# Seven own-buffer column pieces and seeded dot products at the end of a streaming matrix-vector kernel with a running record count

## Chip, cores, metric

One core of one Trainium2 chip. The metric is the device time of one execution in microseconds. PE is TensorE, PEld its weight load, DVE is VectorE, ACT is ScalarE, POOL is GpSimd, SP issues the input loads.

## The reference

```python
B, S, D = 8, 2048, 4096
x: (B, S, D) float32, w: (D, 1) float32

proj = (x @ w).squeeze(-1)                 # (8, 2048)
cm = np.maximum.accumulate(proj, axis=1)   # running maximum
is_record = (proj >= cm)
return np.cumsum(is_record, axis=1)        # how many records so far
```

The input is 268.4 MB and each element is used once. Whatever else the kernel does, it has to pull that much through the DMA engines.

## The kernel before

Positions lie on partitions. Seven groups of 256 positions are loaded as tiles of 128 partitions by 2 positions (32 KB per partition, 4 MB per load), the last 256 positions as two groups of 128 (2 MB per load), each group for all eight batches. DVE makes a dot product per position with one instruction that multiplies and sums. A transpose on PE then brings the sums of a group to a row per batch, and three short DVE instructions do the scan.

```python
const_pool = ctx.enter_context(tc.tile_pool(name="const", bufs=1))
xpool = ctx.enter_context(tc.tile_pool(name="xpool", bufs=4))     # [P, 2*D] each, 32 KB per partition
...
LAST = {                                  # how the last two tiles are cut into column pieces
    1: [(1024, D), (0, 1024)],
    0: [(2048, D), (768, 2048), (0, 768)],
}
...
parts = const_pool.tile([P, 32], FP32)    # the last small tile allocated before the x buffers
...
        if not split:                     # all groups but the last
            for j in range(r):
                xs = x_sb[:, j * D : (j + 1) * D]
                nc.vector.scalar_tensor_tensor(
                    out=xs, in0=xs, scalar=1.0, in1=w_sb, op0=ALU.mult, op1=ALU.mult,
                    accum_out=sum_v[:, j * B + b : j * B + b + 1])
        else:                             # last group: DVE takes columns below 3072 ...
            ...
            if c1 > CV:                   # ... Pool and ACT the 1024 above
                xp = x_sb[:, CV - c0 : c1 - c0]
                nc.gpsimd.tensor_mul(out=xp, in0=xp, in1=w_sb[:, CV:c1])
                nc.scalar.activation(out=xp, in_=xp, func=ACTF.Copy, accum_out=sum_p[:, b : b + 1])
            if b and c1 < D:
                nc.gpsimd.tensor_add(out=sum_v[:, b : b + 1], in0=sum_v[:, b : b + 1], in1=acc_v)
...
                for k, (m, lhs) in enumerate(mms):     # transposes; the piece sums of batch 0 are added here
                    nc.tensor.matmul(out=ps[:m, j : r * P : r], lhsT=lhs, rhs=identity, ...)
```

Every piece of the last two tiles goes into one of the same four 32 KB buffers, so a piece cannot be loaded before an older tile has been worked off.

Of the kernel before, what the change touches and what calls it, by code (L numbers as in the profile page):

```python
# [12 lines left out]
FP32 = mybir.dt.float32  # L13
ALU = mybir.AluOpType
ACTF = mybir.ActivationFunctionType
# [3 lines left out]
@with_exitstack  # L19
def kernel(  # L20
    ctx: ExitStack,
    tc: tile.TileContext,
    x: bass.AP,
    w: bass.AP,
    out: bass.AP,
):






    nc = tc.nc
    P = 128
    B, S, D = x.shape
    CV = 3072
    NW = 8
    WC = D // NW

    const_pool = ctx.enter_context(tc.tile_pool(name="const", bufs=1))  # L40
    xpool = ctx.enter_context(tc.tile_pool(name="xpool", bufs=4))
    gpool = ctx.enter_context(tc.tile_pool(name="gpool", bufs=2))
    wpsum = ctx.enter_context(
        tc.tile_pool(name="wpsum", bufs=1, space=bass.MemoryType.PSUM)
    )
    psum_pool = ctx.enter_context(
        tc.tile_pool(name="psum", bufs=2, space=bass.MemoryType.PSUM)
    )

    LAST = {  # L50
        1: [(1024, D), (0, 1024)],
        0: [(2048, D), (768, 2048), (0, 768)],
    }
    groups = []
    s = 0
    while s < S:
        r = 2 if s + 4 * P <= S else 1
        groups.append((s, r))
        s += r * P
    NG = len(groups)  # L60
    loads = []
    for g in range(NG):
        for b in reversed(range(B)):
            cuts = LAST.get(b) if g == NG - 1 else None
            for c0, c1 in cuts or [(0, D)]:
                loads.append((g, b, c0, c1))

    def start_load(i):
        g, b, c0, c1 = loads[i]
        s, r = groups[g]  # L70
        x_sb = xpool.tile([P, 2 * D], FP32, name="x_sb")
        if r == 2:
            nc.sync.dma_start(
                out=x_sb,
                in_=x[b, s : s + 2 * P, :].rearrange("(p r) d -> p (r d)", r=2),
            )
        else:
            nc.sync.dma_start(out=x_sb[:, : c1 - c0], in_=x[b, s : s + P, c0:c1])
        return x_sb

    AHEAD = 2
    first = [start_load(i) for i in range(AHEAD)]

    w_row = const_pool.tile([NW, WC], FP32)
    nc.scalar.dma_start(out=w_row, in_=w.rearrange("(k c) one -> k (c one)", k=NW))
    identity = const_pool.tile([P, P], FP32)
    make_identity(nc, identity)
    w_v = wpsum.tile([P, CV], FP32)
    w_sb = const_pool.tile([P, D], FP32)
    for k in range(NW):  # L90
        c = k * WC
        if c < CV:
            dst = w_v[:, c : c + WC]
        else:
            dst = psum_pool.tile([P, WC], FP32, name="ps")
        nc.tensor.matmul(  # L96
            out=dst, lhsT=identity[:NW, k : k + 1].to_broadcast([NW, P]),
            rhs=w_row, start=True, stop=True,
        )
        nc.scalar.copy(out=w_sb[:, c : c + WC], in_=dst)  # L100

    neg = const_pool.tile([B, 2 * P], FP32)
    zero = const_pool.tile([B, 2 * P], FP32)
    nc.gpsimd.memset(neg, NEG)
    nc.gpsimd.memset(zero, 0.0)
    parts = const_pool.tile([P, 32], FP32)

    state = {"cm": NEG, "cnt": 0.0}

    def scan_group(g, ps):  # L110
        s, r = groups[g]
        n = r * P
        cm = gpool.tile([B, n], FP32, name="cm")
        rec = gpool.tile([B, n], FP32, name="rec")
        cnt = gpool.tile([B, n], FP32, name="cnt")
        nc.vector.tensor_tensor_scan(  # L116
            out=cm, data0=ps[:B, :n], data1=neg[:, :n], initial=state["cm"],
            op0=ALU.max, op1=ALU.max,
        )
        nc.vector.tensor_tensor(out=rec, in0=ps[:B, :n], in1=cm, op=ALU.is_ge)  # L120
        nc.vector.tensor_tensor_scan(  # L121
            out=cnt, data0=rec, data1=zero[:, :n], initial=state["cnt"],
            op0=ALU.add, op1=ALU.add,
        )
        state["cm"] = cm[:, n - 1 : n]
        state["cnt"] = cnt[:, n - 1 : n]
        eng = nc.sync if g == NG - 1 else nc.scalar
        eng.dma_start(out=out[:, s : s + n], in_=cnt)

    pending = None  # L130
    npart = 0
    late = []
    for i, (g, b, c0, c1) in enumerate(loads):
        s, r = groups[g]
        x_sb = first[i] if i < AHEAD else start_load(i)
        split = g == NG - 1
        if b == B - 1:
            sum_v = gpool.tile([P, 2 * B], FP32, name="sum_v")
            sum_p = gpool.tile([P, B], FP32, name="sum_p")
        if not split:  # L140
            for j in range(r):
                xs = x_sb[:, j * D : (j + 1) * D]
                nc.vector.scalar_tensor_tensor(  # L143
                    out=xs, in0=xs, scalar=1.0, in1=w_sb,
                    op0=ALU.mult, op1=ALU.mult,
                    accum_out=sum_v[:, j * B + b : j * B + b + 1],
                )
        else:
            acc_v = sum_v[:, b : b + 1]
            if c1 < D:  # L150
                acc_v = parts[:, npart : npart + 1]
                late.append((b, acc_v))
                npart += 1
            v1 = min(c1, CV)
            if v1 > c0:
                xs = x_sb[:, : v1 - c0]
                nc.vector.scalar_tensor_tensor(  # L157
                    out=xs, in0=xs, scalar=1.0, in1=w_v[:, c0:v1],
                    op0=ALU.mult, op1=ALU.mult, accum_out=acc_v,
                )  # L160
            if c1 > CV:
                xp = x_sb[:, CV - c0 : c1 - c0]
                nc.gpsimd.tensor_mul(out=xp, in0=xp, in1=w_sb[:, CV:c1])  # L163
                nc.scalar.activation(  # L164
                    out=xp, in_=xp, func=ACTF.Copy, accum_out=sum_p[:, b : b + 1]
                )
            if b and c1 < D:
                nc.gpsimd.tensor_add(
                    out=sum_v[:, b : b + 1], in0=sum_v[:, b : b + 1], in1=acc_v
                )  # L170
        if pending is not None and b == B - 3:
            scan_group(*pending)
            pending = None
        if b == 0 and c0 == 0:
            ps = psum_pool.tile([P, WC], FP32, name="ps")
            for j in range(r):
                mms = [(B, sum_v[:, j * B : (j + 1) * B])]
                if split:
                    mms.append((B, sum_p))
                    mms.extend((1, col) for lb, col in late if lb == 0)  # L180
                for k, (m, lhs) in enumerate(mms):
                    nc.tensor.matmul(  # L182
                        out=ps[:m, j : r * P : r], lhsT=lhs, rhs=identity,
                        start=k == 0, stop=k == len(mms) - 1,
                    )
            pending = (g, ps)
    scan_group(*pending)
# [30 lines left out]
```

## Time and profile before

| what | before | read from |
|---|---|---|
| time | 634.01 us median of 4 (633.93 to 634.09) | runs |
| span of the profiled execution | 632.0 us | page |
| input | 268.4 MB at about 432 GB/s | slice table |
| one 128x4096 dot product | 4417 ns, 120 of them | groups |
| step from one 4 MB load to the next | 9.67 us (median) | completions in the trace |
| time of one 32 KB packet | 1213 ns (7139 of 7168 packets) | packets in the trace |
| last whole 2 MB load landed | 615.30 us | completions |
| last piece landed | 626.13 us | completions |
| last matmul ends | 628.38 us | timeline |

The page of the kernel before: the 40 equal slices of the span (the DMA row is the mean busy share of the 16 DMA engines in tenths) and the group of the full-width dot products (busy us, mean ns | idle before).

```profile
DVE  0699999989899889999899898998989989999976
DMA  9999999999999999999999999999999999999994
GB/s 370 438 438 436 438 436 432 431 432 431 431 432 431 431 431 432 431 431 436 433 436 438 438 436 430 432 436 431 431 431 432 431 433 433 427 431 431 431 429 178
...
L143 DVE SCALAR_TENSOR_TENSOR x_sb<-x_sb,w_sb 128x4096 f32<-128x4096 f32 x120 | 524.6, 4417 | 50.4 <-DMA x_sb<-in_x_dram 29.1
```

The DMA engines are full from start to end. DVE is busy 90% of the time but is not the limit: two dot products take 8.7 us (they start 4.35 us apart where DVE waits for nothing) of a load step of 9.67.

The tail of the kernel before, from the chain that ended last (start us, length us, what; "issue" is time in which nothing is seen to be waited for, DVEq is DVE's sequencer):

```profile
619.02 6.22 DMA x_sb<-in_x_dram
625.25 0.03 issue
625.27 0.05 DVEq L157
625.33 0.04 issue
625.37 0.83 DVE x_sb L157
626.20 0.58 issue
626.78 0.97 DVE x_sb L157 x3
627.75 0.04 issue
627.79 0.60 PE ps L182 x2
628.39 0.03 issue
628.42 0.48 DVE cm L116
```

The stretches of the tail before (length, then busy us with the count of instructions for PE, PEld, DVE, ACT and POOL in this order, granted clock, DMA share, GB/s):

```profile
620.00:622.00 2.00, 0.00 (x0) 0.00 (x0) 2.00 (x3) 0.49 (x1) 1.47 (x1) 1.00 0.95 348
622.00:624.00 2.00, 0.00 (x0) 0.00 (x0) 1.73 (x4) 0.66 (x2) 1.34 (x2) 1.00 0.23 88
624.00:626.00 2.00, 0.59 (x2) 0.12 (x2) 0.65 (x3) 0.82 (x1) 1.15 (x1) 1.00 0.54 171
```

The DMA engines run dry at 622 to 624 us, because the last two pieces waited for a buffer (issued at 619.02 and 622.68 us). But the mean over 16 engines hides something. A load has 16 completions, and DVE starts on it after the last: the piece whose last completion is at 622.67 us, 1.93 us after the median one, has its dot product start at 622.79 us. In the trace, 15 engines report within 0.5 us of each other up to 362 us and within 1.0 us from 431 us on, and one reports later, by about 0.35 us at first, 1.0 us from 139 us on, and 1.9 us from 392 us on. I call this the lag below; it is the last completion of a load minus the median one. The steps in it follow 8 KB packets of a separate queue that fetches instructions, seen at 133.4 and 386.1 us. By the records of the trace these are 129 DVE instructions apart. From 139 us on, the packets of the late engine form one chain with the fetches of 133.4 and 386.1 us, each starting where the one before ends: a fetch takes 0.31 us in it, and the 32 KB packet after it 1.75 us instead of 1.21. This one slow engine, not the mean, paces each load, and in the tail of the kernel before it hardly idled: its packets, each starting where the one before ends, run without a gap from 617 us to a third fetch at 623.87 us.

### The profile page before, as it was taken

The page shows a single profiled execution, that of the slowest core. Times are in us where ns is not written, and L with a number is a line of the kernel's source. Part 1 is how long each engine was busy: PE and PEld are TensorE (multiplying, and loading weights), DVE is VectorE, ACT ScalarE, POOL GpSimd, SP SyncE. Part 2 cuts the span into 40 slices and gives each one's busy share as a digit, 9 for nine tenths or more (in the row PEclk, how much of TensorE's full clock was granted, in tenths as well). Part 3 has the DMA queues.
Part 4 walks back from the last instruction along what each step waited for, and adds up shares of the span by engine and source line. Part 5 has one row for each costly group of instructions (what it writes and reads, how often), then busy time and mean ns, then how long its engine had stood idle before and what let it go on. Part 6 is the DMA issues. An engine that isn't in the chain of part 4 may idle for free.

```text
span 632.0 us, 725 instructions
## 1 busy us (share of the span) xinstructions
PE 26.6 (4%) x54; PEld 6.5 (1%) x54; DVE 567.2 (90%) x289; ACT 15.2 (2%) x25; POOL 21.5 (3%) x17
## 2 busy tenths in 40 slices
PE   7200000000000000000000000000000000000001
PEld 2000000000000000000000000000000000000000
DVE  0699999989899889999899898998989989999976
ACT  3000000000000000000000000000000000000122
POOL 0000000000000000000000000000000000000344
DMA  9999999999999999999999999999999999999994
GB/s 370 438 438 436 438 436 432 431 432 431 431 432 431 431 431 432 431 431 436 433 436 438 438 436 430 432 436 431 431 431 432 431 433 433 427 431 431 431 429 178
DMA packets 10964, 268.56 MB, mean 425 GB/s; under 512 B 1280, under 2 KB 1352, under 8 KB 1744
## 3 DMA queue, kind: packets, MB, share of 16 engines
q1 hardware_dynamic: 10816, 268.44, 98.7%
q10 hardware_dynamic: 144, 0.08, 0.0%
q14 instruction: 4, 0.03, 0.0%
HBM read 268.45 MB, written 0.07 MB: 425 GB/s over the span
## 4 chain that ended last, share of the span: by engine, by line
DMA 56%; DVE 36%; issue 4%; PE 3%; ACT 1%; POOL 0%; DVEq 0%; POOLq 0%; SPq 0%
DMA x_sb<-in_x_dram 55%; DVE x_sb L143 34%; PE w_v L96 2%; DVE x_sb L157 1%; PE ps L96 1%; ACT w_sb L100 0%; DVE cnt L121 0%; POOL x_sb L163 0%; DVE cm L116 0%; PE ps L182 0%; DMA w_row<-in_w_dram 0%; DVE rec L120 0%; ACT x_sb L164 0%; DVEq L143 0%; DVEq L157 0%
## 5 line engine op out<-in xcount | busy, mean ns | idle before, releaser
L143 DVE SCALAR_TENSOR_TENSOR x_sb<-x_sb,w_sb 128x4096 f32<-128x4096 f32 x120 | 524.6, 4417 | 50.4 <-DMA x_sb<-in_x_dram 29.1
L163 POOL TENSOR_TENSOR x_sb<-x_sb,w_sb 128x1024 f32<-128x1024 f32 x8 | 20.2, 2522 | 601.9 <-DMA x_sb<-in_x_dram 598.0
L182 PE MATMUL ps<-identity,sum_v 128*8 128x128 f32 x32 | 9.4, 398 | 594.7 <-DVE x_sb L143 563.9
L157 DVE SCALAR_TENSOR_TENSOR x_sb<-x_sb,w_v 128x3072 f32<-128x3072 f32 (+4 forms) x11 | 26.9, 2474 | 5.7 <-DMA x_sb<-in_x_dram 5.4
L164 ACT ACTIVATE x_sb<-x_sb 128x1024 f32<-128x1024 f32 x8 | 8.5, 1057 | 595.9 <-DMA out_dram<-cnt 574.4
L96 PE MATMUL w_v<-w_row,identity 8*128 8x512 f32 x12 | 12.2, 1121 | 5.2 <-ACT w_sb L100 2.7
L116 DVE TENSOR_TENSOR_SCAN cm<-ps,cm,neg 8x256 f32<-8x256 f32 (+1 forms) x8 | 5.4, 669 | 4.9 <-PE ps L182 4.9
L143 DVE DVE_READ_ACCUMULATOR x_sb<-x_sb,w_sb 128x1 f32 x120 | 9.6, 80 | 0.0
L182 PEld LDWEIGHTS ps<-identity,sum_v 128*8 128x8 f32 x32 | 1.8, 90 | 603.4 <-issue 434.2
L121 DVE TENSOR_TENSOR_SCAN cnt<-rec,cnt,zero 8x256 f32<-8x256 f32 (+1 forms) x8 | 5.8, 725 | 0.3
L100 ACT COPY w_sb<-w_v 128x512 f32<-128x512 f32 x6 | 3.5, 586 | 11.7 <-PE w_v L96 11.7
L120 DVE TENSOR_TENSOR rec<-ps,cm 8x256 f32<-8x256 f32 (+1 forms) x9 | 3.4, 382 | 0.3
L96 PE MATMUL ps<-w_row,identity 8*128 8x512 f32 x4 | 3.6, 1056 | 0.0
L96 PEld LDWEIGHTS w_v<-w_row,identity 8*128 8x128 f32 x12 | 3.1, 310 | 12.5 <-ACT w_sb L100 9.5
L164 ACT ACTIVATION_READ_ACCUMULATOR x_sb<-x_sb 128x1 f32 x8 | 1.5, 187 | 0.0
L116 DVE TENSOR_TENSOR_SCAN cm<-ps,neg 8x256 f32<-8x256 f32 x1 | 0.7, 678 | 0.8 <-PE ps L182 0.8
L96 PEld LDWEIGHTS ps<-w_row,identity 8*128 8x128 f32 x4 | 1.3, 332 | 2.1 <-issue 2.1
L100 ACT ACT_TABLE_LOAD x1 | 1.3, 1283 | 1.4 <-PEq L202 1.4
L100 ACT COPY w_sb<-ps 128x512 f32<-128x512 f32 x2 | 1.2, 586 | 2.2 <-PE ps L96 2.2
L182 PE MATMUL ps<-identity,parts 128*1 128x128 f32 x4 | 1.2, 395 | 0.3 <-DVE x_sb L157 0.3
L157 DVE DVE_READ_ACCUMULATOR x_sb<-x_sb,w_v 128x1 f32 x11 | 0.9, 79 | 0.0
L121 DVE TENSOR_TENSOR_SCAN cnt<-rec,zero 8x256 f32<-8x256 f32 x1 | 0.7, 678 | 0.1
(12 smaller groups left out, 2.6 us busy)
## 6 DMA issues: line engine op xcount, KB each, us to landing
x_sb<-in_x_dram SPq DMA_DIRECT2D x56, 4096.0 KB, 29.5
x_sb<-in_x_dram SPq DMA_DIRECT2D x14, 2048.0 KB, 13.6
x_sb<-in_x_dram SPq DMA_DIRECT2D x1, 1536.0 KB
x_sb<-in_x_dram SPq DMA_DIRECT2D x1, 1024.0 KB, 8.5
x_sb<-in_x_dram SPq DMA_DIRECT2D x1, 640.0 KB
x_sb<-in_x_dram SPq DMA_DIRECT2D x1, 512.0 KB
x_sb<-in_x_dram SPq DMA_DIRECT2D x1, 384.0 KB
out_dram<-cnt ACTq DMA_DIRECT2D x7, 8.0 KB
```

What stands on the lines that cost most here:

```text
L96: nc.tensor.matmul(out=dst, lhsT=identity[:NW, k : k + 1].to_broadcast([NW, P]), rhs=w_row, start=True, stop=True,)
L100: nc.scalar.copy(out=w_sb[:, c : c + WC], in_=dst)
L116: nc.vector.tensor_tensor_scan(out=cm, data0=ps[:B, :n], data1=neg[:, :n], initial=state["cm"], op0=ALU.max, op1=ALU.max,)
L120: nc.vector.tensor_tensor(out=rec, in0=ps[:B, :n], in1=cm, op=ALU.is_ge)
L121: nc.vector.tensor_tensor_scan(out=cnt, data0=rec, data1=zero[:, :n], initial=state["cnt"], op0=ALU.add, op1=ALU.add,)
L143: nc.vector.scalar_tensor_tensor(out=xs, in0=xs, scalar=1.0, in1=w_sb, op0=ALU.mult, op1=ALU.mult, accum_out=sum_v[:, j * B + b : j * B + ...
L157: nc.vector.scalar_tensor_tensor(out=xs, in0=xs, scalar=1.0, in1=w_v[:, c0:v1], op0=ALU.mult, op1=ALU.mult, accum_out=acc_v,)
L163: nc.gpsimd.tensor_mul(out=xp, in0=xp, in1=w_sb[:, CV:c1])
L164: nc.scalar.activation(out=xp, in_=xp, func=ACTF.Copy, accum_out=sum_p[:, b : b + 1])
L182: nc.tensor.matmul(out=ps[:m, j : r * P : r], lhsT=lhs, rhs=identity, start=k == 0, stop=k == len(mms) - 1,)
```

## The change

Its intent: let the last two tiles' loads run without waiting for a buffer, cut them so that little is left to do after the last byte, chain the partial sums of a batch through a seed so that no additions are left over, take Pool and ACT in for the last 256 positions instead of 128, and close with one group of transposes. Cut to its core:

```diff
-    CV = 3072
-    NW = 8
-    WC = D // NW
+    WC = 512
+    NW = D // WC
+    CV = D - WC
@@
+    lpool = ctx.enter_context(tc.tile_pool(name="lpool", bufs=1))
@@
-        tc.tile_pool(name="psum", bufs=2, space=bass.MemoryType.PSUM)
+        tc.tile_pool(name="psum", bufs=1, space=bass.MemoryType.PSUM)
@@
-    LAST = {
-        1: [(1024, D), (0, 1024)],
-        0: [(2048, D), (768, 2048), (0, 768)],
-    }
+    PIECES = {                              # (first column, first column of Pool and ACT, end)
+        1: [(1280, 3072, D), (0, 768, 1280)],
+        0: [(2816, 3584, D), (1792, 2432, 2816), (1024, 1536, 1792),
+            (512, 1024, 1024), (0, 512, 512)],
+    }
+    WHOLE = [(0, 2816, D)]
@@ start_load
-            nc.sync.dma_start(out=x_sb[:, : c1 - c0], in_=x[b, s : s + P, c0:c1])
+            if c1 - c0 == D:
+                x_sb = xpool.tile([P, 2 * D], FP32, name="x_sb")[:, :D]
+            else:
+                x_sb = lpool.tile([P, c1 - c0], FP32, name=f"x_{b}_{c0}")
+            nc.sync.dma_start(out=x_sb, in_=x[b, s : s + P, c0:c1])
@@
-    parts = const_pool.tile([P, 32], FP32)
+    NP = max(len(p) for p in PIECES.values()) - 2
+    parts = const_pool.tile([P, NP, B], FP32)
+    nc.gpsimd.memset(parts, 0.0)
+    acc = const_pool.tile([P, 16], FP32)
@@
+    def dot(xs, ws, seed, dst):
+        nc.vector.tensor_tensor_reduce(
+            out=xs, in0=xs, in1=ws, scale=1.0, scalar=seed,
+            op0=ALU.mult, op1=ALU.add, accum_out=dst,
+        )
@@ every dot product, seeded by the sum of the piece before
-                nc.vector.scalar_tensor_tensor(..., accum_out=...)
+            dot(x_sb[:, : v - c0], w_v[:, c0:v], seed, dst)
+            seed = dst
@@ the transposes of the last group
-                    mms.append((B, sum_p))
-                    mms.extend((1, col) for lb, col in late if lb == 0)
+                    lhs.insert(0, sum_p)
+                if g == NG - 1:
+                    lhs[1:1] = [parts[:, k, :] for k in range(NP)]
```

More of the change, by code (lines that the diff above doesn't have):

```diff
@@ L46 @@
     psum_pool = ctx.enter_context(
-        tc.tile_pool(name="psum", bufs=2, space=bass.MemoryType.PSUM)
+        tc.tile_pool(name="psum", bufs=1, space=bass.MemoryType.PSUM)
     )
-    LAST = {
-        1: [(1024, D), (0, 1024)],
-        0: [(2048, D), (768, 2048), (0, 768)],
+    PIECES = {
+        1: [(1280, 3072, D), (0, 768, 1280)],
+        0: [
+            (2816, 3584, D),
+            (1792, 2432, 2816),
+            (1024, 1536, 1792),
+            (512, 1024, 1024),
+            (0, 512, 512),
+        ],
     }
+    WHOLE = [(0, 2816, D)]
     groups = []
@@ L63 @@
         for b in reversed(range(B)):
-            cuts = LAST.get(b) if g == NG - 1 else None
-            for c0, c1 in cuts or [(0, D)]:
-                loads.append((g, b, c0, c1))
+            if groups[g][1] == 2:
+                loads.append((g, b, 0, D, D))
+            else:
+                for c0, v, c1 in (PIECES.get(b) if g == NG - 1 else None) or WHOLE:
+                    loads.append((g, b, c0, v, c1))
     def start_load(i):
-        g, b, c0, c1 = loads[i]
+        g, b, c0, _, c1 = loads[i]
         s, r = groups[g]
-        x_sb = xpool.tile([P, 2 * D], FP32, name="x_sb")
         if r == 2:
+            x_sb = xpool.tile([P, 2 * D], FP32, name="x_sb")
             nc.sync.dma_start(
@@ L77, in start_load @@
         else:
-            nc.sync.dma_start(out=x_sb[:, : c1 - c0], in_=x[b, s : s + P, c0:c1])
+            if c1 - c0 == D:
+                x_sb = xpool.tile([P, 2 * D], FP32, name="x_sb")[:, :D]
+            else:
+                x_sb = lpool.tile([P, c1 - c0], FP32, name=f"x_{b}_{c0}")
+            nc.sync.dma_start(out=x_sb, in_=x[b, s : s + P, c0:c1])
         return x_sb
@@ L130 @@
     pending = None
-    npart = 0
-    late = []
-    for i, (g, b, c0, c1) in enumerate(loads):
+    nacc = 0
+    for i, (g, b, c0, v, c1) in enumerate(loads):
         s, r = groups[g]
         x_sb = first[i] if i < AHEAD else start_load(i)
-        split = g == NG - 1
         if b == B - 1:
             sum_v = gpool.tile([P, 2 * B], FP32, name="sum_v")
-            sum_p = gpool.tile([P, B], FP32, name="sum_p")
-        if not split:
-            for j in range(r):
-                xs = x_sb[:, j * D : (j + 1) * D]
-                nc.vector.scalar_tensor_tensor(
-                    out=xs, in0=xs, scalar=1.0, in1=w_sb,
-                    op0=ALU.mult, op1=ALU.mult,
-                    accum_out=sum_v[:, j * B + b : j * B + b + 1],
-                )
-        else:
-            acc_v = sum_v[:, b : b + 1]
-            if c1 < D:
-                acc_v = parts[:, npart : npart + 1]
-                late.append((b, acc_v))
-                npart += 1
-            v1 = min(c1, CV)
-            if v1 > c0:
-                xs = x_sb[:, : v1 - c0]
-                nc.vector.scalar_tensor_tensor(
-                    out=xs, in0=xs, scalar=1.0, in1=w_v[:, c0:v1],
-                    op0=ALU.mult, op1=ALU.mult, accum_out=acc_v,
-                )
-            if c1 > CV:
-                xp = x_sb[:, CV - c0 : c1 - c0]
-                nc.gpsimd.tensor_mul(out=xp, in0=xp, in1=w_sb[:, CV:c1])
-                nc.scalar.activation(
-                    out=xp, in_=xp, func=ACTF.Copy, accum_out=sum_p[:, b : b + 1]
-                )
-            if b and c1 < D:
-                nc.gpsimd.tensor_add(
-                    out=sum_v[:, b : b + 1], in0=sum_v[:, b : b + 1], in1=acc_v
-                )
@@ new lines @@
+            if r == 1:
+                sum_p = gpool.tile([P, B], FP32, name="sum_p")
+        if r == 2:
+            for j in range(2):
+                dot(
+                    x_sb[:, j * D : (j + 1) * D], w_sb, 0.0,
+                    sum_v[:, j * B + b : j * B + b + 1],
+                )
+        else:
+            if c1 == D:
+                seed, piece = 0.0, 0
+            dst = sum_v[:, b : b + 1]
+            if c0:
+                dst = acc[:, nacc : nacc + 1]
+                nacc += 1
+            dot(x_sb[:, : v - c0], w_v[:, c0:v], seed, dst)
+            seed = dst
+            if v < c1:
+                xp = x_sb[:, v - c0 :]
+                nc.gpsimd.tensor_mul(out=xp, in0=xp, in1=w_sb[:, v:c1])
+                pacc = (
+                    parts[:, piece - 1, b : b + 1] if piece else sum_p[:, b : b + 1]
+                )
+                nc.scalar.activation(out=xp, in_=xp, func=ACTF.Copy, accum_out=pacc)
+                piece += 1
@@ L176 @@
             for j in range(r):
-                mms = [(B, sum_v[:, j * B : (j + 1) * B])]
-                if split:
-                    mms.append((B, sum_p))
-                    mms.extend((1, col) for lb, col in late if lb == 0)
-                for k, (m, lhs) in enumerate(mms):
+                lhs = [sum_v[:, j * B : (j + 1) * B]]
+                if r == 1:
+                    lhs.insert(0, sum_p)
+                if g == NG - 1:
+                    lhs[1:1] = [parts[:, k, :] for k in range(NP)]
+                for k, l in enumerate(lhs):
                     nc.tensor.matmul(
-                        out=ps[:m, j : r * P : r], lhsT=lhs, rhs=identity,
-                        start=k == 0, stop=k == len(mms) - 1,
+                        out=ps[:B, j : r * P : r], lhsT=l, rhs=identity,
+                        start=k == 0, stop=k == len(lhs) - 1,
                     )
```

## The prediction

> **What bounds the kernel now.** The slice table shows the DMA row at 9 in 39 of 40 slices, about 432 GB/s; 268.4 MB at that rate is 621 us of the 632.0 us span. DVE is busy 90%, but its groups show 4417 ns per 128x4096 dot product (a pitch of 4.35 us in the timeline) against about 9.7 us per 4 MB tile of two dot products, so it has roughly 1 us of slack per tile. Everything before the tail belongs to the input stream; only the tail can move.
>
> **The tail before** (timeline, chain of waits, landings in the trace). The last loads are five pieces in recycled 4 MB buffers. The DMA queue's own waits show the last two piece loads issued only at 619.0 and 622.7 us; the DMA share falls to 0.08 at 622.5 to 623.5. The 1280 piece lands at 625.25, the last at 626.13. DVE then works 1.49 + 0.95 us to 627.75, the last fp32 matmul takes 0.6, the three scan steps 1.3, output and end 2.3: 632.0.
>
> The refill is not all loss. Of the 16 completions of each load, 15 come about 1.9 us before the last: one DMA engine paces every load. Its lag jumps by 0.7 us near 139 us and by 0.95 near 392 us, after 8 KB instruction fetches at 133.4 and 386.1; a third comes at 623.9. They are 128 Vector instructions apart. That engine was idle only about 0.15 us in the tail.
>
> **What the change does.**
> - scalar_tensor_tensor becomes tensor_tensor_reduce with a seed. [...] I expect the same for the new operation, 4.35 to 4.6 us: hidden. The accumulator read (0.08 us) stays.
> - Pool and ACT take 1280 columns in the last two groups: by 2.36 us per 1024 I estimate 2.9 us Pool and 1.3 us ACT per tile, DVE 3.1 us, all below the 4.87 us of a 2 MB load. Hidden. [...]
> - One spare PSUM bank less: the start of DVE moves from 21.3 to about 22.3 us; four buffers hide it.
> - Seven pieces in own buffers: the refill gap goes. The pacing engine would end about 625.0, but the third fetch (about the same instruction count) now falls into its running stream, costing an estimated 0.3 to 0.95 us. Last landing 625.5 to 626.3.
> - After it: DVE 0.7 us for 512 columns, with the seed chaining two such pieces, about 1.1 us; but Pool's queue (2.4, 1.3, 1.3, 1.0, 0.7 us), ACT and two parts matmuls (one of them all zeros) bring the last matmul's end to about 2.2 us after the landing: 628.1 instead of 628.39.
>
> **Predicted: 633.7 us, range 632.2 to 635.0.** Faster by over 2%: 0.01; within 2%: 0.94; slower by over 2%: 0.05.
>
> **Right if** the DMA row stays at 9 to the end, dot products stay near 4.4 us, the last landing is within 0.6 us of 626.1, and the last group's final matmul waits for ACT/Pool parts about as long as for DVE. **Wrong step shown by** dot products over 4.75 us [...], DMA gaps in the last 10 us, Pool near 3 us or more per 1024, or a changed pacing lag.
>
> **What would make it wrong.** A tensor_tensor_reduce at half rate; seeded pieces that stall on the accumulator round trip; if the fetch misses the pacing engine or its cost hides, 632.5.

Passages that no trace or run of this case showed are cut out of it, and the cuts are marked. They hold no term of its sum: 628.1 us for the end of the last matmul, plus the 5.6 us that follow it in the kernel before (634.01 less 628.38), make the 633.7 us. Its "the same" for the new dot product means the 4417 ns of the old one; that the new one would match was my expectation, without a run behind it at that time. The risks that it names under "what would make it wrong" were conjectures; measured afterwards, the new product took 4418 ns, and the seeded one of 128x768 took 1014 ns against 955 ns with a constant seed.

## The result

The changed kernel takes 636.58 us median (636.47 to 636.71, 4 runs) against 634.01 us (633.93 to 634.09). The ratio is 1.0041, 95% interval 1.0023 to 1.0058. A ratio here is the mean time of one kernel's runs over that of the other's in the same rounds, so it is not quite the ratio of the medians. The change costs 2.6 us, where about 0.3 us of gain was predicted, and the time lies outside the predicted range of 632.2 to 635.0 us.

The page of the changed kernel, the lines that answer to those of before:

```profile
DVE  0599999989899889999899898998989989997767
DMA  9999999999999999999999999999999999999994
GB/s 373 448 432 432 430 432 430 430 428 430 430 430 430 430 432 432 432 432 436 440 432 434 430 430 428 430 430 430 430 430 430 432 432 434 425 428 427 427 424 182
...
L132 DVE CUSTOM_DVE_ANT_0 x_sb<-x_sb,w_sb 128x4096 f32<-128x4096 f32 x112 | 489.8, 4418 | 52.9 <-DMA x_sb<-in_x_dram 30.4
```

The new dot product costs the same 4.42 us. The DMA row is as full as before, but the GB/s row reads 430 in most slices where it read 431 to 438. Half a per cent is easy to overlook in such a row, and a DMA share of 9 says nothing about it, since a slow packet is a busy packet.

It is plain in the timeline if the same load is looked up in both kernels. This is the first dot product on the last of the 56 loads of 4 MB, first in the kernel before (start us, us, engine line operation, shapes, [idle before, and what ended it]):

```profile
547.23 4.42 DVE L143 SCALAR_TENSOR_TENSOR x_sb<-x_sb,w_sb 128x4096 f32<-128x4096 f32 x1 [0.90 <-DMA x_sb<-in_x_dram]
```

and then in the changed kernel:

```profile
549.73 4.42 DVE L132 CUSTOM_DVE_ANT_0 x_sb<-x_sb,w_sb 128x4096 f32<-128x4096 f32 x1 [0.95 <-DMA x_sb<-in_x_dram]
```

In both, DVE had been idle for 0.9 us and was released by the load. So the input is 2.5 us late before the changed tail has begun.

The chain at the end of the changed kernel:

```profile
604.92 22.17 DMA x_1792_506<-in_x_dram
627.09 0.03 issue
627.12 0.02 DVEq L132
627.14 0.09 issue
627.22 0.88 DVE x_1792_506 L132
628.10 0.02 DVE acc L132
...
629.78 0.75 DVE x_0_519 L132
630.52 0.02 DVE sum_v L132
630.54 0.04 issue
630.59 0.61 PE ps L201 x2
631.20 0.02 issue
631.22 0.48 DVE cm L143
```

And the stretches of its tail:

```profile
622.00:624.00 2.00, 0.00 (x0) 0.00 (x0) 1.77 (x2) 0.74 (x2) 2.00 (x1) 1.00 1.01 396
624.00:626.00 2.00, 0.00 (x0) 0.00 (x0) 1.14 (x3) 1.53 (x3) 1.49 (x3) 1.00 0.93 353
626.00:628.00 2.00, 0.00 (x0) 0.00 (x1) 1.62 (x3) 1.07 (x4) 2.00 (x2) 1.00 0.11 41
```

The hole of 0.23 in the DMA share is gone, as intended: the pieces were issued 16 to 23 us before they landed. What that brought, and what the whole span lost, adds up as follows.

| stretch | before | after | difference |
|---|---|---|---|
| start to the landing of the last whole load | 615.30 | 618.29 | +2.99 |
| from there to the landing of the last piece | 10.83 | 11.09 | +0.26 |
| from there to the end of the last matmul | 2.25 | 1.81 | -0.44 |
| from there to the end of the span | 3.61 | 3.50 | -0.11 |
| span | 632.0 | 634.7 | +2.7 |

The first row is the question. Its loads, their sizes and their order are the same in both kernels.

### The profile page after: what moved, and what is told of

It reads as the page before. It is cut to its first block, busy times and chain, and to the rows that moved or that the text cites. A ratio compares the mean times of both kernels' runs of the same rounds, so it can differ in the third digit from the quotient of the medians.

```text
span 634.7 us, 788 instructions
## 1 busy us (share of the span) xinstructions
PE 27.9 (4%) x58; PEld 6.9 (1%) x58; DVE 557.9 (88%) x293; ACT 28.8 (5%) x47; POOL 52.0 (8%) x28
## 4 chain that ended last, share of the span: by engine, by line
DMA 60%; DVE 31%; issue 3%; PE 3%; ACT 1%; POOL 1%; SPq 0%; DVEq 0%; POOLq 0%
DMA x_sb<-in_x_dram 57%; DVE x_sb L132 30%; DMA x_1792_506<-in_x_dram 3%; PE w_v L114 2%; POOL x_sb L183 1%; ACT w_sb L118 1%; ACT x_sb L187 0%; DVE cm L143 0%; DMA w_row<-in_w_dram 0%; PE ps L114 0%; SPq L96 0%; PE ps L201 0%; DVE cnt L148 0%; DVE rec L147 0%; DVE sum_v L132 0%
## 5 line engine op out<-in xcount | busy, mean ns | idle before, releaser
L132 DVE CUSTOM_DVE_ANT_0 x_sb<-x_sb,w_sb 128x4096 f32<-128x4096 f32 x112 | 489.8, 4418 | 52.9 <-DMA x_sb<-in_x_dram 30.4
L183 POOL TENSOR_TENSOR x_sb<-x_sb,w_sb 128x1280 f32<-128x1280 f32 x14 | 44.2, 3157 | 575.4 <-DMA x_sb<-in_x_dram 575.1
L132 DVE CUSTOM_DVE_ANT_0 x_sb<-x_sb,w_v 128x2816 f32<-128x2816 f32 x14 | 43.0, 3078 | 12.0 <-DMA x_sb<-in_x_dram 12.0
L187 ACT ACTIVATE x_sb<-x_sb 128x1280 f32<-128x1280 f32 x14 | 17.8, 1269 | 581.2 <-POOL x_sb L183 574.2
L114 PE MATMUL w_v<-w_row,identity 8*128 8x512 f32 x14 | 14.3, 1122 | 6.0 <-ACT w_sb L118 3.4
L132 DVE DVE_READ_ACCUMULATOR2_ANT sum_v<- 128x1 f32 x128 | 10.2, 79 | 0.0
L148 DVE TENSOR_TENSOR_SCAN cnt<-rec,cnt,zero 8x256 f32<-8x256 f32 (+1 forms) x8 | 8.3, 1038 | 0.2
L183 POOL TENSOR_TENSOR x_1280_491<-x_1280_491,w_sb 128x1024 f32<-128x1024 f32 x1 | 2.4, 2352 | 0.4 <-DMA x_1280_491<-in_x_dram 0.4
L132 DVE CUSTOM_DVE_ANT_0 x_1280_491<-x_1280_491,w_v 128x1792 f32<-128x1792 f32 x1 | 2.0, 2020 | 0.2 <-DMA x_1280_491<-in_x_dram 0.2
L114 PE MATMUL ps<-w_row,identity 8*128 8x512 f32 x2 | 1.9, 1056 | 0.0
L132 DVE CUSTOM_DVE_ANT_0 x_0_496<-x_0_496,w_v,acc 128x768 f32<-128x768 f32 x1 | 1.0, 1014 | 0.6 <-DMA x_0_496<-in_x_dram 0.6
```

The lines of the kernel that those rows point to most:

```text
L114: nc.tensor.matmul(out=dst, lhsT=identity[:NW, k : k + 1].to_broadcast([NW, P]), rhs=w_row, start=True, stop=True,)
L132: nc.vector.tensor_tensor_reduce(out=xs, in0=xs, in1=ws, scale=1.0, scalar=seed, op0=ALU.mult, op1=ALU.add, accum_out=dst,)
L148: nc.vector.tensor_tensor_scan(out=cnt, data0=rec, data1=zero[:, :n], initial=state["cnt"], op0=ALU.add, op1=ALU.add,)
L183: nc.gpsimd.tensor_mul(out=xp, in0=xp, in1=w_sb[:, v:c1])
```

## The experiments

The packets in the trace gave the first theory. In the kernel before, nearly all 32 KB packets take exactly 1213 ns; in the changed one nearly all take 1211 to 1224, most often 1216 and 1224. On average 32 KB packets went from 1214.7 to 1219.0 ns, those of 16 KB from 611.0 to 615.8, those of 4 KB from 159.0 to 162.0. The extra is 3 to 5 ns per packet whatever its size, so it does not grow with the bytes. It looks like a fixed cost per packet; where in the packet it arises was not shown. It is nearly enough for the loss: before the last whole load lands, one engine takes 448 packets of 32 KB and 112 of 16 KB, and at 4.3 and 4.8 ns more for each this makes, by an estimate from these means, 2.5 of the 2.99 us. The compiled programs give the place of the x buffers in a partition:

```
before   x buffers start at byte 37632 = 147 * 256
after    x buffers start at byte 37664 = 147 * 256 + 32     (parts 96 + acc 64 bytes, where parts took 128)
```

Theory A: the start of the destination, 32 bytes past a multiple of 256, lengthens every packet. Theory B: the new dot product instruction disturbs the writes of the loads. Theory C: the pieces and their buffers do it. The first four runs shared one chip.

### e1: the changed kernel with the buffers back on a multiple of 256

```diff
-    acc = const_pool.tile([P, 16], FP32)
+    acc = const_pool.tile([P, 8], FP32)
```

> The changed kernel with its accumulator tile cut from 16 to 8 columns, so that every input buffer starts 32 bytes earlier in its partition, at a multiple of 256 bytes as in the kernel before; no instruction changes. Theory A (the start address of the buffers slows every DMA packet): the 32 KB packets go back from a median of 1216 ns to 1213 ns, the step between landings of 4 MB loads from 9.725 to 9.68 us, the time from 636.6 to 633.2-633.9 us (ratio to the kernel before about 0.999). Theory B (the new dot product disturbs the DMA writes) and theory C (the seven pieces and their buffers): no change, about 636.6 us (1.004).

Measured: correct, 633.19 us (633.14 to 633.52) against 634.04 us, ratio 0.9989 (0.9976 to 1.0001). Packets are at 1213 ns again (7135 of 7168), the median step is 9.67 us. The same dot product as above, in e1:

```profile
547.41 4.43 DVE L132 CUSTOM_DVE_ANT_0 x_sb<-x_sb,w_sb 128x4096 f32<-128x4096 f32 x1 [0.91 <-DMA x_sb<-in_x_dram]
```

Against 549.73 us that is 2.3 us, from a tile that is 32 bytes smaller and no other edit. Theories B and C fall for this part: every new instruction and every piece is still there.

### e2: the kernel before with its buffers 32 bytes later

```diff
-    parts = const_pool.tile([P, 32], FP32)
+    parts = const_pool.tile([P, 40], FP32)
```

> The kernel before with its parts tile widened from 32 to 40 columns, so that its input buffers start 32 bytes later, where those of the changed kernel start; no instruction changes. Theory A: packets of 1213 ns become about 1216 ns, the landing step about 9.725 us, the time about 637.0 us (ratio about 1.0047). Theories B and C: 634.0 us, ratio 1.000.

Measured: correct, 636.74 us (636.60 to 636.95), ratio 1.0044 (1.0031 to 1.0057). Packets are most often 1216 and 1224 ns, the median step 9.72 us, and the same dot product starts late here too:

```profile
549.90 4.43 DVE L143 SCALAR_TENSOR_TENSOR x_sb<-x_sb,w_sb 128x4096 f32<-128x4096 f32 x1 [0.94 <-DMA x_sb<-in_x_dram]
```

So 32 bytes alone turn the kernel before into one as slow as the changed kernel.

### e3: the old dot product in the changed kernel

```diff
-                dot(x_sb[:, j * D : (j + 1) * D], w_sb, 0.0, sum_v[...])
+                xs = x_sb[:, j * D : (j + 1) * D]
+                nc.vector.scalar_tensor_tensor(
+                    out=xs, in0=xs, scalar=1.0, in1=w_sb,
+                    op0=ALU.mult, op1=ALU.mult, accum_out=sum_v[...])
```

> The changed kernel with scalar_tensor_tensor put back for the 112 full-width dot products; buffers stay 32 bytes past a multiple of 256. Theory B: the landing step returns to 9.68 us and the time to about 633.7 us (ratio 0.9995). Theory A: the step stays at 9.725 us and the time at about 636.6 us (1.004); the dot products keep 4.42 us in both.

Measured: correct, 636.57 us (636.41 to 636.72), ratio 1.0041 (1.0028 to 1.0053); packets 1216 and 1224 ns, step 9.72 us. This is the time of the changed kernel. The new instruction is neutral.

### e4, e5, e6: how far past a multiple of 256

The same `acc` tile with 24, 40 and 72 columns, which puts the buffers 64, 128 and 256 bytes past the place of before. e5 and e6 ran later, with e7 and e8.

> The changed kernel with the accumulator tile widened to 24 columns: input buffers start 64 bytes past a multiple of 256. Theory A with a boundary of 256 bytes: still slow, step about 9.72 us, about 636 us or more. Theory A with a boundary of 64 bytes only: as fast as e1, about 633.5 us. Theory B or C: 636.6 us.

Measured: correct, 636.13 us (635.82 to 636.27), ratio 1.0032 (1.0019 to 1.0046).

> The changed kernel with the accumulator tile of 40 columns: input buffers start 128 bytes past a multiple of 256 (and 64- and 128-byte aligned). If the boundary that matters is 256 bytes: still slow, packets above 1213 ns, 635.5 to 636.6 us. If 128 bytes is enough: as e1, 633.2 us, packets 1213 ns.

Measured: correct, 635.97 us (635.51 to 636.11), ratio 1.0027 (1.0013 to 1.0041).

> The accumulator tile of 72 columns: input buffers start at a multiple of 512 bytes (those of the kernel before and of e1 start 256 past one). If 256 bytes is the boundary: as e1, 633.2 us and packets of 1213 ns. If 512 bytes mattered: shorter packets and below 633 us. If what counts is not alignment but the mere size or place of the small tiles: some other time.

Measured: correct, 633.16 us (633.02 to 633.41), ratio 0.9985 (0.9972 to 0.9997).

| buffers start at | kernel | mean 32 KB packet, ns | most frequent | median step, us | time, us |
|---|---|---|---|---|---|
| 256k | before | 1214.7 | 1213 | 9.67 | 634.01 |
| 256k | e1 | 1214.4 | 1213 | 9.67 | 633.19 |
| 256k + 32 | after | 1219.0 | 1216 | 9.72 | 636.58 |
| 256k + 32 | e2, before shifted | 1218.7 | 1216 | 9.72 | 636.74 |
| 256k + 64 | e4 | 1218.1 | 1215 | 9.72 | 636.13 |
| 256k + 128 | e5 | 1218.1 | 1218 | 9.71 | 635.97 |
| 256k (a multiple of 512) | e6 | 1214.4 | 1213 | 9.68 | 633.16 |

Offsets of 32, 64 and 128 bytes past a multiple of 256 are all slow; the starts at a multiple of 256 are fast, and a multiple of 512 brings no more. Other offsets were not run. e6 also makes the tile larger than in any slow variant, so the size of the small tiles is not what counts.

In these runs the extra does not grow with the size of the packet or with the offset: 3 to 5 ns for packets of 4, 16 and 32 KB at an offset of 32 bytes, and about 4 ns per 32 KB packet at each of the three offsets (means of 1218.1 to 1219.0 ns against 1214.4 to 1214.7). Why that is so, and what happens inside the DMA engine, was not shown and stays open.

### e7: one instruction fetch more

The prediction's other claim was that instruction fetches cost time through the pacing engine. In e1 they stand at these times (8 KB packets of the instruction queue within the span):

```
e1   133.57   365.99   386.27   605.15   619.23 us
e7    10.94   134.06   366.88   386.76   605.16   619.72 us
```

Those at 133.6, 386.3 and 619.2 us are taken to be DVE's, as they are 129 and 130 DVE instructions apart in the trace's records; after each of them the lag rises. After those at 366 and 605 us it does not. e7 adds 128 tiny instructions to e1 while DVE has nothing to do anyway:

```diff
+    for _ in range(128):
+        nc.vector.memset(acc[:, 7:8], 0.0)
```

> e1 with 128 one-column Vector memsets ahead of the first dot product, while Vector waits for w anyway. Theory of the fetches (every 128 Vector instructions one 8 KB fetch goes through the DMA engine that paces the loads and costs it about 0.95 us for good): one fetch more in the stream, the lag of the last completion grows to about 3.9 us in the tail, and the time rises by 0.9 to 1.0 us, to about 634.15 us. If fetches are harmless: 633.2 us.

Measured: correct, 634.01 us (633.85 to 634.11), ratio 0.9998 (0.9985 to 1.0010). e6 above, of the same rounds and as well aligned as e1, took 633.16 us: the fetch costs 0.85 us. It shows at 10.94 us, and the later ones stay where they were, within 0.9 us: 128 more instructions bring exactly one fetch more. The lag is 2.46 us ahead of the tail, where e6 has 1.84, and the last landing is at 626.69 us, where e6 has 625.97. So a fetch does cost time although no engine is seen to wait for it. The lag grew by 0.6 us rather than the 0.95 expected (and is 3.3 us in the tail, not 3.9); the last landing moved by 0.7 us.

### e8, e9, e11: keeping the fetch out of the tail

In e1 the third fetch falls into the tail, at 619.23 us, and the lag rises from 1.97 to about 2.9 us there. If DVE has fewer instructions ahead of the tail, that fetch comes later. e8, like e9 and e11, starts from e1. It counts the records of the first eight groups in one scan instead of eight:

```diff
-        rec = gpool.tile([B, n], FP32, name="rec")
-        cnt = gpool.tile([B, n], FP32, name="cnt")
+        rec = rec_all[:, s : s + n]
@@ scan_group
+        if g < NG - 2:
+            return
+        c = 0 if g == NG - 2 else s
+        n = s + n - c
+        cnt = const_pool.tile([B, n], FP32, name=f"cnt{g}")
```

> e1 with the counting scans of the first eight groups put together in one (seven Vector instructions fewer; same outputs). The third fetch of Vector then comes 6 to 8 us later in the tail, at about 625 to 628 us; the pacing engine sends its last data by about 625 us without it. Theory of the fetches: where it falls behind the last data, the last landing comes 0.95 us earlier and the time is about 632.3 us; where it still hits the last packets, between 632.3 and 633.2 us. If fetches are harmless: 633.2 us. Rival: the long scan of 1792 positions (an estimate of 3.8 us by the 2.1 ns per position of the 256-position scans) delays the dot products of the last group, and the time rises.

Its 2.1 ns per position fits the slope of the traced count scans of the kernel before: 0.74 us for 256 positions, 0.47 us for 128.

Measured: correct, 633.36 us (632.91 to 633.84), ratio 0.9988 (0.9976 to 1.0001); no clear difference from e1. The fetch moved to 623.93 us and still met the last two pieces: the lag stayed near 1.6 us up to the fifth piece and was 2.55 us at the sixth. The last landing was at 626.12 us.

e9 moves it further. It takes e8, loads batch 1 of the last group whole, and gives two full-width dot products to Pool and ACT.

```diff
-        1: [(1280, 3072, D), (0, 768, 1280)],
@@
             for j in range(2):
+                if j and (g, b) in ((2, 4), (4, 4)):
+                    xp = x_sb[:, D:]
+                    nc.gpsimd.tensor_mul(out=xp, in0=xp, in1=w_sb)
+                    nc.scalar.activation(out=xp, in_=xp, func=ACTF.Copy,
+                                         accum_out=sum_v[:, B + b : B + b + 1])
+                    continue
```

> e8 taken further: one counting scan for the first eight groups, batch 1 of the last group loaded whole instead of in two pieces, and two of the 112 full-width dot products given to Pool and ACT, so that Vector has 13 instructions fewer than in e1 and its third fetch is due after the last input data. Theory of the fetches: the lag of the last completion stays where it is before the tail (1.6 to 2.0 us) through the last load, the last landing comes near 625.2 us instead of 626.2, and the time is about 632.2 us (0.9972), against 633.2 us of e1. If fetches are harmless: 633.2 us. If the two products on Pool hold up Vector or the loads: above 633.2 us, with gaps in the DMA row near them.

Measured: correct, 633.78 us (633.58 to 633.84), ratio 0.9996 (0.9982 to 1.0009). The landing did what the theory says: the fetch came at 625.23 us, the lag stayed at 1.6 us through the tail, and the last piece landed at 624.91 us, 1.1 us earlier than in e10. The time did not follow, because I had given DVE a new backlog. Its timeline in e9:

```profile
620.05 3.09 DVE L132 CUSTOM_DVE_ANT_0 x_sb<-x_sb,w_v 128x2816 f32<-128x2816 f32 x1 [1.78 <-DMA x_sb<-in_x_dram]
623.06 0.08 DVE L132 DVE_READ_ACCUMULATOR2_ANT sum_v<- 128x1 f32 x1
623.06 0.95 DVE L132 CUSTOM_DVE_ANT_0 x<-x,w_v 128x768 f32<-128x768 f32 x1
...
626.56 0.75 DVE L132 CUSTOM_DVE_ANT_0 x<-x,w_v,acc 128x512 f32<-128x512 f32 x1
```

The whole tile of batch 1 keeps DVE until 623.06 us, while the next piece had landed at 621.43. From there on DVE works without a gap and is done at 627.31 us, 2.4 us after the last landing. This is one reason for cutting batch 1 in two.

e10 is e1 again, on the same chip as e9:

> e1 again, on the same chip and in the same rounds as e9: 633.2 us (0.9989), last landing near 626.2 us, lag of the last completion rising from about 2.0 to 2.9 us at the second load of the tail.

Measured: 633.22 us (633.14 to 633.43), ratio 0.9988 (0.9975 to 1.0000), last landing 625.97 us; the lag rises from 1.68 to 2.62 us at the second piece.

e11 is e9 with batch 1 in two pieces again:

> e8 with two of the 112 full-width dot products given to Pool and ACT, but batch 1 of the last group in two pieces again, so that Vector starts the last pieces on time (in e9 it was the whole tile of batch 1 that made Vector late). Vector has 11 instructions fewer than in e1. Theory of the fetches: the third fetch comes after the last data (about 626 us), the last landing near 625.2 us, Vector's last dot product ends about 1.2 us after it, and the time is about 632.3 us. If an earlier landing is worth nothing: 633.2 us, as e1; if the two products on Pool cost something: above 633.2 us.

Measured: correct, 632.68 us (632.54 to 632.92) against 633.96 us, ratio 0.9981 (0.9968 to 0.9995). The fetch is at 624.84 us and touches only the last piece; the lag is 1.8 us up to the sixth piece and 2.0 at the last. The last landing is at 625.41 us, the last dot product ends 0.9 us later:

```profile
625.60 0.75 DVE L133 CUSTOM_DVE_ANT_0 x<-x,w_v,acc 128x512 f32<-128x512 f32 x1
626.27 0.08 DVE L133 DVE_READ_ACCUMULATOR2_ANT sum_v<- 128x1 f32 x1
626.41 0.26 PEld L214 LDWEIGHTS ps<-identity,sum_v 128*8 128x8 f32 x2 [0.17 <-DVE sum_v L133]
```

It is the best version here and beats both kernels, by 0.2% over the kernel before. It ran on another job than e10, so the 0.5 us between them (632.68 and 633.22 us, against 633.96 and 633.92 us of the kernel before) is read across two jobs. e11 also takes two full-width products off DVE; that the fetch and not this brings the gain is read from the lag (1.8 to 2.0 us in the tail, where e10 has 2.5 to 2.6 from the second piece on), and no run keeps the two apart.

## Why the prediction was wrong

**The step that failed** is the sentence "Everything before the tail belongs to the input stream; only the tail can move." The stream moved by 2.99 us, which is the whole loss and more. I had looked at what the change does to the work of each engine, found every addition hidden, and took the rate of the loads as given because their code was untouched. But the change also moved the buffers they write to by 32 bytes, and each of the 32 KB packets got a few ns longer. e1 and e2 show this from both sides: 32 bytes off the changed kernel take the loss away, 32 bytes added to the kernel before bring it. The signs that the prediction named for a wrong step do not point here: dot products stayed at 4.42 us, the DMA row at 9, and the lag ahead of the tail was 2.05 us against 1.92.

Point by point:

- *The new dot product at 4.35 to 4.6 us, hidden.* Right: 4418 ns against 4417 ns, and e3 shows that it makes no difference to the time (636.57 us with the old product, 636.58 us with the new one). A seed read from the sum just made cost about 0.06 us in the changed kernel: 1014 ns against 955 ns with a constant seed, one instruction each, both for 128x768.
- *Pool, ACT and the later start of DVE hidden.* Right as far as seen: Pool took 2.9 us per 1280 columns in the last group against a load step of 4.9 us, DVE started at 22.50 us instead of 21.31, and with the buffers aligned (e1) the last whole load landed at 615.42 us against 615.30 us.
- *The refill gap goes, but the pacing engine gains little from it.* Right. The hole in the DMA row went, and the tail's loads took 11.09 us instead of 10.83.
- *The third fetch now falls into the tail's running loads and costs 0.3 to 0.95 us.* Right in mechanism: the lag rises from 2.07 to 3.02 us between the first and the second piece, and e11 gets some of it back by moving the fetch. But "now" was wrong: the fetch had met the tail of the kernel before as well (at 623.87 us, lag from 1.93 to 2.75), so at least a part of this cost is in both kernels. With the buffers aligned the last piece lands at 626.21 us (e1) against 626.13. It was called "about the same instruction count"; the place of the fetch turned out to be something one can choose.
- *Last landing 625.5 to 626.3 us.* Wrong for the changed kernel (629.38 us), right for e1 (626.21 us).
- *Last matmul ends 2.2 us after the landing, bound by Pool and ACT.* The size was 1.81 us, and the reason was wrong: PE had finished with the parts and waited 0.62 us for DVE. The fetch in the tail probably left Pool the time to work off its queue, which the estimate had not included: in e11, where it meets only the last piece, PE waits 0.17 us.
- *633.7 us.* With the buffers aligned the same change gives 633.19 us, inside the predicted range. The sum outside the stream stands, in part by luck: the last matmul of e1 ends at 628.11 us, as forecast, but as 626.21 + 1.90 instead of about 625.9 + 2.2, two errors of 0.3 us that cancel. The change does bring about 0.8 us when its buffers lie right. By the interval (0.9976 to 1.0001, in e10 0.9975 to 1.0000, in e6 0.9985 with 0.9972 to 0.9997) that is a small gain, barely clear of none.

About 0.2 us of that gain is in neither kernel's span. In the profiled executions the time less the span is 1.98 us for the kernel before, 2.12 us for e2, 2.12 for e9 and 2.02 for e11; it is 1.79 us for the changed kernel and 1.77 to 1.78 us for e1, e7, e8 and e10. The first four show one more instruction fetch after their last instruction, the others do not. No run tests this by itself, so it stays an observation.

What stays open: why a start off a 256-byte boundary costs about the same at 32, 64 and 128 bytes; and why a fetch costs sometimes 0.6 and sometimes 0.95 us of lag.

## What to carry to other kernels

In a kernel bound by its loads, look at where the buffers start, not only at what is loaded: 32 bytes more of small tiles allocated ahead of them cost 0.4% here, without one instruction being slower in the list of groups. Let the large buffers start at a multiple of 256 bytes per partition by padding (32 KB packets took 1214 to 1215 ns on average here, against 1218 to 1219 with starts 32, 64 or 128 bytes past it), and look the address up in the compiled program. Allocating them first is not enough by itself: the first tile of both kernels starts at byte 16512 = 64 * 256 + 128. When a change should leave a stage alone, compare the time of the same load in both traces at the end of that stage before reasoning about the next one; and read a full DMA by the last of its 16 completions, since a busy share can't tell a slow packet from a fast one (the DMA row reads 9 in 39 of 40 slices in both kernels).
